# Half of a long depthwise convolution: three taps and the bias moved from VectorE to ScalarE and GpSimd, and a planner that holds back ScalarE table switches

## The chip, the cores and the metric

The kernel runs on one core of one Trainium2 chip. A core has five engines that run their own instruction queues beside each other: TensorE (PE in the profile, with PEld for its weight loads), VectorE (DVE), ScalarE (ACT), GpSimd (POOL) and SyncE (SP, which here only issues DMA transfers). The metric is the device time of one execution in microseconds. The time before is the median of three runs. The prediction is for the median after the change.

## The reference

The reference is a two-layer network in float32 on a sequence of 256 tokens with 1024 channels. Each layer is a feed-forward half step, a mixer, and another feed-forward half step, each between two RMS norms. The feed-forward part is `(silu(gate) * up) @ w2` with an inner width of 2816. The mixer of the second layer is a dilated attention in three patterns. The mixer of the first layer, the hybrid, is the one that the change touches:

```python
def conformer_conv(u, w_dw, b_dw, ln_g, ln_b):
    val, gate = jnp.split(u, 2, axis=-1)
    hid = causal_depthwise_conv(val * jax.nn.sigmoid(gate), w_dw, b_dw)
    return jax.nn.silu(layer_norm(hid, ln_g, ln_b))
...
def conv_ssd_mixer(...):
    proj = u @ w_in
    conv_in, z, xbc, dt_raw = jnp.split(proj, [s0, s1, s2], axis=-1)
    ya = conformer_conv(conv_in, ...)
    yb = mamba2_ssd(z, xbc, dt_raw, ...)
    return jnp.concatenate([ya, yb], axis=-1) @ w_out
```

The long convolution has 31 taps on each of 1024 channels: output at time t is the bias plus the sum over s from 0 to 30 of weight(30 - s) times the input at time t - s. The state space part (`mamba2_ssd`) has a short convolution of 4 taps with Silu behind it, on x, B and C; step sizes from a softplus; decays, which are exponentials of cumulated sums; and a gate `silu(z)`.

## The kernel before

**The matrix products.** Weights come from HBM in units of 128 x 2048 float32 (tile `raw`). ScalarE copies each unit into a rounded part (`wh`, type fp32r) and VectorE or GpSimd subtracts to get the rest (`wl`). Activations are split in the same way (`x`, `s`). A product is then three TensorE matmuls: high by high, high by low, low by high. All of these splits are in the queues of ScalarE, VectorE and GpSimd beside the other work. In the hybrid stage 17 units have their low part made on GpSimd (`GPSIMD_UNITS`).

**The order of the work.** The kernel's methods do not issue instructions. A `Recorder` notes each operation with what it reads and writes, and a planner puts them in an order for each engine before anything is issued. So every instruction in the profile has one line, L617, and an operation is known by its tiles (`wh<-raw` is a split, `t<-cv,chan,t` a convolution tap into PSUM bank `t`). The planner (`schedule`, L398) makes six turns. In each, `one_schedule` (L478) goes through time with costs for each operation (`cost`, L636) and chooses for each engine, in `choose` (L508), among the operations whose inputs are done and whose buffers can be had: of those that can start within `LOOK` (100 ns for VectorE and ScalarE) of the earliest, the one with the lowest rank. In the first turn the rank is the place in the program, shifted by `moved(...)`. In later turns it is a due time that `look_back` (L428) works out backwards from TensorE's order of the turn before. The turn with the shortest planned span is kept. Operations that start before `FIXED`, 35 us, keep their time of the first turn as their due time.

ScalarE's functions lie in tables: Exp, Silu and Sigmoid each need a table of their own, Copy, Identity and Square none (`TABLES`, L633). When an operation needs another table than the one loaded, an ACT_TABLE_LOAD stands ahead of it. The planner adds 1294 ns to its cost, and 3000 ns (`TABLE_TIME`) to its due time or 200 places to its rank.

**Buffers.** Tiles are of kinds, each with a fixed count. The kind `s`, 128 x 512 float32 in SBUF, has 17 buffers; `cv`, which holds the gated input of the long convolution (`glu`) and its result, has 5; in PSUM there are 4 banks `a`, 2 `w`, 1 `t` and 1 `c`. Buffers of a kind are given out in the order in which the program makes its tiles: a later one gets a buffer only when enough are free for the earlier ones without.

**The hybrid stage** (`hybrid`, L1178). The gated input of the long convolution is made as four tiles `glu[0]` to `glu[3]` of 2 x 128 channels by 256 tokens, the first two with tokens as rows and a transpose, the last two by `gated_feat` (L981), all with Sigmoid. In between stand the step sizes, which need Exp (`step_sizes`, L1139). `long_conv` (L1197) has two halves, `glu[0]` and `glu[1]`, then `glu[2]` and `glu[3]`. In each half the banks `t` and `c` hold the sums of one tile each. ScalarE starts a block with tap 1 and the bias (Identity with scale and bias from memory, 255 columns, L1207) and sets column 0 to the bias. VectorE adds the taps 2 to 30 in place in PSUM, one instruction `scalar_tensor_tensor` for each tap and block of 128 channels, and last tap 0, which writes the result to a `cv` tile (L1215). That is 30 VectorE instructions for each of the eight blocks.

Beside it run `xbc_pair` (L1223: projection, four taps of the short convolution, Silu) for B (`xbc_pair(4)`), C (`xbc_pair(5)`) and the four parts of x; `grow` (L1269) and `decays` (L1272: ScalarE scales a triangular matrix by each head's step, `s<-order,m`; a matmul cumulates; Exp follows, with a second small Exp `m<-a` for `left` in the first token tile); `gate_z` (Silu); and the products of the state space part. Behind both come `ln_half` (L1320: transposes of the convolution's result, then the layer norm) and the output projection.

Of the kernel before, what the change touches and what calls it, by code (L numbers as in the profile page):

```python
# [14 lines left out]
AF = mybir.ActivationFunctionType  # L15
ALU = mybir.AluOpType
# [3 lines left out]
P = 128  # L20
D = 1024
DFF = 2816
SEQ = 256
# [23 lines left out]
SECOND = 30  # L47
POOL_PIECE = 512
ON_POOL = (1, 1, 1)
CONV = (2000,1600)  # L50
GATE = 200
CONV_INIT = (-500, -100)
# [156 lines left out]
H_DW, H_DB, H_LG, H_LB, H_SW, H_SB = 0, 248, 256, 264, 272, 320  # L209
# [89 lines left out]
class Recorder:  # L299
# [81 lines left out]
    def together(self):  # L381
# [3 lines left out]
        head, rest = self.ops[at], self.ops[at + 1 :]  # L385
        head.cost += SWITCH
        for o in rest:
# [90 lines left out]
    def one_schedule(self):  # L478
# [18 lines left out]
        best = {}  # L497
        stale = set(free)

        def place_time(buf):  # L500
            kind = buf.kind
            ahead = 0
            for b in kind.bufs[kind.first : buf.index]:
                ahead += b.slot is None
            times = sorted(t for t in kind.free_at if t is not None)
            return times[ahead] if len(times) > ahead else None

        def choose(e):  # L508
            found = []
            low = None  # L510
            for o in cands[e]:
                s = max(free[e], ready[o.index])
                rank = o.rank if o.due is None else o.due
                if e == "scalar" and o.table and o.table != table:
                    rank += TABLE_RANKS if o.due is None else TABLE_TIME
                for b in o.bufs:
                    if b.slot is None:
                        t = place_time(b)
                        if t is None:
                            break  # L520
                        s = max(s, t + GAP)
                else:
                    found.append((rank, s, o))
                    if low is None or s < low:
                        low = s
            if low is None:
                return None
            return min((f for f in found if f[1] <= low + LOOK[e]), key=lambda f: f[:2])

        while len(order) < len(ops):  # L530
            for e in stale:
                best[e] = choose(e)
            stale = set()
            picks = [(b[1], e) for e, b in best.items() if b]
            assert picks, "no operation can start"
            s, e = min(picks)
            o = best[e][2]
            cands[e].remove(o)
            stale.add(e)
            for b in o.bufs:  # L540
# [38 lines left out]
            for u in users[o.index]:  # L579
                n = ops[u]  # L580
# [40 lines left out]
TURNS = 6  # L621
FIXED = 35000.0
TABLE_TIME = 3000.0
SWITCH = 280.0
TABLE_LOAD = 1294.0
TABLE_RANKS = 200
# [5 lines left out]
LOOK = {"tensor": 50.0, "vector": 100.0, "scalar": 100.0, "gpsimd": 0.0, "sync": 0.0}  # L632
# [71 lines left out]
class Kernel:  # L704
# [473 lines left out]
    def hybrid(self, xT, done):  # L1178
        nc = self.nc
        V = nc.vector  # L1180
        XD, XK, YZ = (nc.gpsimd if x else V for x in ON_POOL)
        chan = self.chan


        glu = []
# [7 lines left out]
        dt, a = self.step_sizes(xT)  # L1193
        for c in (2, 3):
            glu.append(self.gated_feat(xT, AF.Sigmoid))

        def long_conv():  # L1197
            out = []
            for j0 in (0, 2):
                acc = [self.ps([P, 2, SEQ], tag) for tag in "tc"]  # L1200
                part = lambda i: (acc[i % 2][:, i // 2, :], glu[j0 + i % 2][:, i // 2, :], 2 * (j0 + i % 2) + i // 2)
                tap = lambda ct, shift: chan[:, H_DW + ct * 31 + 30 - shift : H_DW + ct * 31 + 31 - shift]
                with nc.moved(CONV_INIT[j0 // 2]):
                    for i in range(4):
                        a, x, ct = part(i)
                        bias = chan[:, H_DB + ct : H_DB + ct + 1]
                        nc.scalar.activation(a[:, 1:], x[:, : SEQ - 1], AF.Identity, bias=bias, scale=tap(ct, 1))  # L1207
                        nc.scalar.activation(a[:, 0:1], bias, AF.Copy)
                o = [self.slot([P, 2, SEQ], tag="cv") for _ in range(2)]
                with nc.moved(CONV[j0 // 2]):  # L1210
                    for s in (*range(2, 31), 0):
                        for i in range(4):
                            a, x, ct = part(i)
                            to = a[:, s:] if s else o[i % 2][:, i // 2, :]
                            nc.vector.scalar_tensor_tensor(out=to, in0=x[:, : SEQ - s], scalar=tap(ct, s), in1=a[:, s:], op0=ALU.mult, op1=ALU.add)  # L1215
                for half in range(2):
                    out += [o[half][:, 0, :], o[half][:, 1, :]]
            return out

        hid = long_conv()  # L1220


# [177 lines left out]
        acc = [None] * NT  # L1400
# [309 lines left out]
```

## Time and profile before

| | |
|---|---|
| median of 3 runs | 1070.03 us (1068.65 to 1070.21) |
| profiled execution | 1070.98 us; its span from first to last instruction 1069.1 us |
| mean granted TensorE clock | 0.997 |
| instructions | 14980 |
| ACT_TABLE_LOAD | 18, mean 1283 ns |
| long convolution taps into bank `t` and into bank `c` | 116 each, mean 464 and 463 ns |
| bytes read from HBM | 194.51 MB, 183 GB/s over the span |

The profile is of one execution. A row of the view of busy time by windows gives the window, its length, then the busy time of PE, PEld, DVE, ACT and POOL with the number of their instructions in brackets, then the granted TensorE clock, the busy share of the DMA engines and GB/s. A row of the timeline gives start, duration, engine, line, operation, the tile written and those read, the shape and how many were merged; in square brackets stands how long the engine was idle before it and what ended that. A row of the groups gives the count behind the x, then busy time in all and the mean of one in ns, then idle time before them and who ended it. Starts of one engine lie closer together than durations, because its instructions overlap. The ends of matmuls are modelled, so a busy TensorE is not always one at its peak.

### The profile page before, as it was taken

What the parts mean: (1) busy time and instruction counts of PE and PEld (TensorE: products, weight loads), DVE (VectorE), ACT (ScalarE), POOL (GpSimd) and SP (SyncE); (2) the same over time, 40 slices, a digit from 0 to 9 for tenths busy, and PEclk for the clock granted to TensorE, in tenths of its full rate; (3) what the DMA queues carried; (4) which work ended last, traced back from release to release, by engine and by line L of the source; (5) the groups of instructions that cost most, each with busy time, mean ns of one, the idle gap of its engine ahead of it and who ended that gap; (6) DMA issues with size and microseconds to landing.
All of it is one profiled execution on the core that took longest, in us unless ns stands there. A gap on an engine that the chain in (4) does not pass through costs nothing.

```text
span 1069.1 us, 14980 instructions
## 1 busy us (share of the span) xinstructions
PE 1047.8 (98%) x5426; PEld 872.7 (82%) x5426; DVE 936.1 (88%) x1533; ACT 707.5 (66%) x1321; POOL 191.6 (18%) x167
## 2 busy tenths in 40 slices
PE   7999999998999999999999999999999999999997
PEld 5888888897877888888888888887888788888886
DVE  5799997789799999999979999998678769999993
ACT  6756666668785676666767666586577658476671
POOL 2410000296896040000003000001000413000000
PEclk9999999999999999999999999999999999999999
DMA  9573657454323532745654466383645232465451
GB/s 334 200 270 122 233 215 258 158 192 164 114 84 118 224 131 98 296 177 217 256 178 157 155 239 238 117 345 142 242 180 196 99 120 66 163 250 215 154 197 39
DMA packets 30633, 196.51 MB, mean 184 GB/s; under 512 B 3680, under 2 KB 4576, under 8 KB 8032
## 3 DMA queue, kind: packets, MB, share of 16 engines
q1 hardware_dynamic: 30560, 195.57, 50.3%
q8 instruction: 42, 0.69, 0.3%
q14 instruction: 31, 0.25, 0.1%
HBM read 194.51 MB, written 1.05 MB: 183 GB/s over the span
## 4 chain that ended last, share of the span: by engine, by line
PE 71%; DVE 2%; ACT 1%; issue 0%; POOL 0%; DVEq 0%; POOLq 0%; ACTq 0%
PE w L617 28%; PE a L617 26%; PE t L617 9%; PE c L617 7%; DVE wl L617 1%; ACT wh L617 0%; DVE s L617 0%; DVE y L617 0%; ACT x L617 0%; DVE h L617 0%; DVE x L617 0%; POOL m L617 0%; ACT junk L617 0%; DVEq L1706 0%; POOLq L1706 0%
## 5 line engine op out<-in xcount | busy, mean ns | idle before, releaser
L617 ACT ACTIVATE wh<-raw 128x512 fp32r<-128x512 f32 (+1 forms) x626 | 452.9, 774 | 157.7 <-DVE raw L617 51.9
L617 DVE TENSOR_TENSOR wl<-raw,wh 128x512 fp32r<-128x512 f32 (+1 forms) x554 | 483.3, 916 | 38.8 <-ACT wh L617 35.8
L617 PE MATMUL a<-wh,s 128*128 128x512 f32 x800 | 257.0, 392 | 0.0
L617 PE MATMUL w<-wh,x 128*128 128x512 f32 x600 | 197.1, 401 | 1.3 <-ACT x L617 0.8
L617 PEld LDWEIGHTS a<-wh,s 128*128 128x128 f32 x800 | 149.6, 188 | 33.6 <-ACT s L617 0.8
L617 PE MATMUL a<-wl,s 128*128 128x512 f32 x400 | 156.3, 391 | 0.0
L617 PE MATMUL w<-x,wh 128*128 128x512 f32 (+1 forms) x512 | 146.3, 352 | 1.3 <-DVE s L617 1.1
L617 POOL TENSOR_TENSOR m<-m,mhalf 128x1 f32<-128x1 f32 x28 | 18.9, 675 | 697.6 <-DVE m L617 697.6
L617 PEld LDWEIGHTS w<-wh,x 128*128 128x128 f32 x600 | 112.7, 190 | 27.0 <-ACT x L617 1.5
L617 PE MATMUL w<-wl,x 128*128 128x512 f32 x300 | 120.0, 401 | 0.0
L617 PE MATMUL w<-x,wl 128*128 128x256 f32 x400 | 112.4, 281 | 0.0
L617 DVE TENSOR_TENSOR raw<-raw,raw 128x1024 f32<-128x1024 f32 (+1 forms) x104 | 109.6, 1083 | 0.0
L617 PEld LDWEIGHTS w<-x,wh 128*128 128x128 f32 x512 | 89.4, 190 | 15.2 <-issue 2.4
L617 POOL TENSOR_TENSOR wl<-raw,wh 128x512 fp32r<-128x512 f32 x72 | 90.9, 1306 | 27.7 <-ACT wh L617 27.3
L617 PEld LDWEIGHTS a<-wl,s 128*128 128x128 f32 x400 | 75.2, 188 | 15.7
L617 PE MATMUL w<-wh,s 128*128 128x512 f32 x264 | 87.3, 391 | 0.0
L617 PEld LDWEIGHTS w<-x,wl 128*128 128x128 f32 x400 | 75.7, 189 | 1.5 <-issue 1.2
L617 PEld LDWEIGHTS w<-wl,x 128*128 128x128 f32 x300 | 57.1, 190 | 12.4 <-issue 0.9
L617 DVE SCALAR_TENSOR_TENSOR t<-cv,chan,t 128x254 f32<-128x254 f32 (+28 forms) x116 | 53.8, 464 | 6.7 <-ACT t L617 6.4
L617 PEld LDWEIGHTS w<-wh,s 128*128 128x128 f32 x264 | 49.6, 188 | 11.2 <-ACT s L617 0.5
L617 PE MATMUL t<-x,wh 128*128 128x512 f32 x160 | 58.0, 397 | 0.0
L617 PE MATMUL c<-x,wh 128*128 128x512 f32 x160 | 56.4, 393 | 0.0
(198 smaller groups left out, 1553.1 us busy)
## 6 DMA issues: line engine op xcount, KB each, us to landing
raw<-in_weights SPq DMA_DIRECT2D x176, 1024.0 KB, 4.9
g<-in_gains SPq DMA_DIRECT2D x11, 512.0 KB, 4.6
raw<-in_weights SPq DMA_DIRECT2D x8, 256.0 KB, 5.9
h<-in_x SPq DMA_DIRECT2D x4, 256.0 KB, 3.3
out<-h SPq DMA_DIRECT2D x4, 256.0 KB, 2.0
g<-in_consts SPq DMA_DIRECT2D x3, 192.0 KB, 2.4
chan<-in_chan SPq DMA_DIRECT2D x1, 170.0 KB, 9.3
order<-in_consts SPq DMA_DIRECT2D x1, 128.0 KB, 9.4
```

Source lines behind the costliest of these rows:

```text
L617: o.ins = f(*[real(a) for a in o.args], **{k: real(a) for k, a in o.kw.items()})
```

## The change

It has two parts.

In the planner, an operation of ScalarE that needs another table than the one loaded, and would start after `FIXED`, counts as starting 400 ns later (`TABLE_HOLD`) where the earliest start is looked for, where those within `LOOK` of it are picked out, and where the engine that goes next is chosen. Its real start is not moved.

In `long_conv`, for the second half alone (`SHARED = (0, 3)`), a new function `shared` makes taps 28, 29 and 30 of both tiles outside VectorE: ScalarE multiplies the shifted input by the tap's weight into an `s` tile (for tap 28 with the bias added, and the first 28 columns set to the bias), and GpSimd adds the three. ScalarE then copies the sum of each tile into its PSUM bank, in place of the start with tap 1. VectorE goes through taps 1 to 27 and 0. The operations of `shared` are moved by 500 places in the first turn. For the first half `n` is 0 and nothing changes.

```diff
--- before.py
+++ after.py
@@ -47,6 +47,8 @@
 SECOND = 30
 POOL_PIECE = 512
 ON_POOL = (1, 1, 1)
+SHARED = (0, 3)
+SHARED_RANKS = (2000, 500)
 CONV = (2000,1600)
 GATE = 200
 CONV_INIT = (-500, -100)
@@ -511,7 +513,9 @@
             for o in cands[e]:
                 s = max(free[e], ready[o.index])
                 rank = o.rank if o.due is None else o.due
+                held_up = 0.0
                 if e == "scalar" and o.table and o.table != table:
+                    held_up = TABLE_HOLD if s > FIXED else 0.0
                     rank += TABLE_RANKS if o.due is None else TABLE_TIME
                 for b in o.bufs:
                     if b.slot is None:
@@ -520,21 +524,21 @@
                             break
                         s = max(s, t + GAP)
                 else:
-                    found.append((rank, s, o))
-                    if low is None or s < low:
-                        low = s
+                    found.append((rank, s, o, s + held_up))
+                    if low is None or s + held_up < low:
+                        low = s + held_up
             if low is None:
                 return None
-            return min((f for f in found if f[1] <= low + LOOK[e]), key=lambda f: f[:2])
+            return min((f for f in found if f[3] <= low + LOOK[e]), key=lambda f: f[:2])
 
         while len(order) < len(ops):
             for e in stale:
                 best[e] = choose(e)
             stale = set()
-            picks = [(b[1], e) for e, b in best.items() if b]
+            picks = [(b[3], e) for e, b in best.items() if b]
             assert picks, "no operation can start"
-            s, e = min(picks)
-            o = best[e][2]
+            e = min(picks)[1]
+            s, o = best[e][1:3]
             cands[e].remove(o)
             stale.add(e)
             for b in o.bufs:
@@ -621,6 +625,7 @@
 TURNS = 6
 FIXED = 35000.0
 TABLE_TIME = 3000.0
+TABLE_HOLD = 400.0
 SWITCH = 280.0
 TABLE_LOAD = 1294.0
 TABLE_RANKS = 200
@@ -1194,25 +1199,55 @@
         for c in (2, 3):
             glu.append(self.gated_feat(xT, AF.Sigmoid))
 
+        def shared(j, at, n, whole):
+            first = None
+            for s in range(at, at + n):
+                a = self.slot([P, 2, SEQ])
+                for b in range(2):
+                    ct = 2 * j + b
+                    tap = chan[:, H_DW + ct * 31 + 30 - s : H_DW + ct * 31 + 31 - s]
+                    if first is None and whole:
+                        bias = chan[:, H_DB + ct : H_DB + ct + 1]
+                        nc.scalar.activation(a[:, b, s:], glu[j][:, b, : SEQ - s], AF.Identity, bias=bias, scale=tap)
+                        nc.scalar.activation(a[:, b, :s], bias.to_broadcast([P, s]), AF.Copy)
+                    else:
+                        nc.scalar.activation(a[:, b, s:], glu[j][:, b, : SEQ - s], AF.Copy, scale=tap)
+                if first is None:
+                    first = a
+                else:
+                    nc.gpsimd.tensor_tensor(out=first[:, :, s:], in0=first[:, :, s:], in1=a[:, :, s:], op=ALU.add)
+            return first
+
         def long_conv():
             out = []
             for j0 in (0, 2):
                 acc = [self.ps([P, 2, SEQ], tag) for tag in "tc"]
                 part = lambda i: (acc[i % 2][:, i // 2, :], glu[j0 + i % 2][:, i // 2, :], 2 * (j0 + i % 2) + i // 2)
                 tap = lambda ct, shift: chan[:, H_DW + ct * 31 + 30 - shift : H_DW + ct * 31 + 31 - shift]
+                n = SHARED[j0 // 2]
+                early = j0 == 2 and n
+                with nc.moved(SHARED_RANKS[j0 // 2]):
+                    some = [shared(j0 + p, 31 - n, n, early) for p in range(2 if n else 0)]
                 with nc.moved(CONV_INIT[j0 // 2]):
-                    for i in range(4):
+                    if early:
+                        for p in range(2):
+                            nc.scalar.activation(acc[p], some[p], AF.Copy)
+                    for i in range(0 if early else 4):
                         a, x, ct = part(i)
                         bias = chan[:, H_DB + ct : H_DB + ct + 1]
                         nc.scalar.activation(a[:, 1:], x[:, : SEQ - 1], AF.Identity, bias=bias, scale=tap(ct, 1))
                         nc.scalar.activation(a[:, 0:1], bias, AF.Copy)
                 o = [self.slot([P, 2, SEQ], tag="cv") for _ in range(2)]
                 with nc.moved(CONV[j0 // 2]):
-                    for s in (*range(2, 31), 0):
+                    for s in (*range(1 if early else 2, 31 - n), 0):
                         for i in range(4):
                             a, x, ct = part(i)
                             to = a[:, s:] if s else o[i % 2][:, i // 2, :]
                             nc.vector.scalar_tensor_tensor(out=to, in0=x[:, : SEQ - s], scalar=tap(ct, s), in1=a[:, s:], op0=ALU.mult, op1=ALU.add)
+                    if some and not early:
+                        for p in range(2):
+                            at = 31 - n
+                            nc.gpsimd.tensor_tensor(out=o[p][:, :, at:], in0=o[p][:, :, at:], in1=some[p][:, :, at:], op=ALU.add)
                 for half in range(2):
                     out += [o[half][:, 0, :], o[half][:, 1, :]]
             return out
```

## The prediction

> **What bounds the kernel now.** I read the page first (busy shares), then busy time by windows, then what TensorE (PE) waits for, then the ScalarE (ACT) order at the place where PE waits.
>
> ```profile
> PE 1047.8 (98%) x5426; PEld 872.7 (82%) x5426; DVE 936.1 (88%) x1533; ACT 707.5 (66%) x1321; POOL 191.6 (18%) x167
> ```
>
> PE is busy 98% of the span. The change takes no matmul away, so it can only gain where PE stands still or runs slowly. The windows say where that is:
>
> ```profile
> 240.00:250.00 10.00, 10.00 (x87) 10.00 (x86) 10.00 (x35) 6.25 (x12) 5.66 (x6) 1.00 0.40 145
> 275.00:280.00 5.00, 5.00 (x45) 5.00 (x44) 4.54 (x13) 2.73 (x6) 4.46 (x4) 1.00 0.06 25
> 330.00:335.00 5.00, 4.37 (x24) 3.42 (x23) 4.45 (x13) 4.39 (x14) 4.67 (x5) 1.00 0.59 208
> 365.00:740.00 375.00, 374.94 (x1781) 310.91 (x1780) 352.49 (x469) 247.65 (x410) 24.16 (x20) 1.00 0.55 201
> ```
>
> ```profile
> 250.00:255.00 5.00, 4.88 (x42) 4.70 (x41) 5.00 (x16) 2.94 (x8) 5.00 (x6) 1.00 0.55 184
> 255.00:260.00 5.00, 3.91 (x34) 3.73 (x33) 5.00 (x14) 5.00 (x16) 5.00 (x6) 1.00 0.59 206
> 260.00:265.00 5.00, 2.79 (x16) 1.70 (x14) 3.35 (x10) 4.94 (x11) 1.26 (x2) 0.99 0.57 213
> 265.00:270.00 5.00, 5.00 (x24) 3.82 (x24) 3.85 (x11) 4.95 (x8) 3.83 (x4) 0.67 0.08 31
> 270.00:275.00 5.00, 3.99 (x23) 2.83 (x23) 4.62 (x13) 3.42 (x10) 3.77 (x4) 1.00 0.52 185
> ```
>
> The columns after the length are busy time of PE, PEld, VectorE (DVE), ACT and GpSimd (POOL), then the granted clock. From 365 to 740 us, two feed-forward stages and more, PE misses 0.06 us of 375: a reordering there can win nothing. The hole is in the hybrid stage, 250 to 275 us: PE misses 0.12 + 1.09 + 2.21 + 0 + 1.01 = 4.43 us, and in 265 to 270 its clock is 0.67, which costs another 5 x 0.33 = 1.65 us. With the 0.63 us at 330 to 335 that makes 6.7 us, the most that the two edits can reach in this stage. In the worst ten microseconds ACT is busy 9.94 of 10. What ended PE's longer waits:
>
> ```profile
> 257.99 0.48 PE L617 MATMUL w<-x,wh 128*128 128x256 f32 x2 [1.09 <-DVE s L617]
> ...
> 262.04 0.44 PE L617 MATMUL a<-ident,s 128*128 128x128 f32 x2 [1.20 <-ACT s L617]
> ...
> 274.20 0.50 PE L617 MATMUL a<-x,wh 128*128 128x256 f32 x2 [1.01 <-ACT m L617]
> ...
> 331.91 0.63 PE L617 MATMUL w<-ident,v 128*128 128x128 f32 x4 [0.63 <-DVE x L617]
> ```
>
> **Edit one, the order: loads of tables.** The new rule holds an ACT operation that would need another table back by 400 ns against one that needs none, and the planner only takes what starts within 100 ns of the earliest. So as long as any operation without a table switch can start within 300 ns, the switch waits, whatever its due time. Before, only 3000 ns were added to its due time. Here is what ACT did in the hole:
>
> ```profile
> 260.06 1.28 ACT L617 ACT_TABLE_LOAD   x1
> 261.36 0.63 ACT L617 ACTIVATE s<-s 128x512 f32<-128x512 f32 x1
> 261.89 1.26 ACT L617 ACTIVATE s<-order,m 128x128 f32<-128x128 f32 x4
> 263.06 0.55 ACT L617 ACTIVATE s<-w,chan 128x256 f32<-128x256 f32 x1
> 263.62 1.28 ACT L617 ACT_TABLE_LOAD   x1
> 264.92 0.18 ACT L617 ACTIVATE m<-a 128x16 f32<-128x16 f32 x1
> 265.00 1.14 ACT L617 ACTIVATE wh<-raw 128x512 fp32r<-128x512 f32 x2
> 266.15 1.28 ACT L617 ACT_TABLE_LOAD   x1
> 267.45 0.63 ACT L617 ACTIVATE s<-s 128x512 f32<-128x512 f32 x1
> 267.99 1.14 ACT L617 ACTIVATE wh<-raw 128x512 fp32r<-128x512 f32 x2
> 269.14 1.28 ACT L617 ACT_TABLE_LOAD   x1
> 270.44 0.60 ACT L617 ACTIVATE s<-a 128x512 f32<-128x512 f32 x1
> ```
>
> Silu for the B channels (261.36), Exp for `grow` (264.92, 0.18 us), Silu for the C channels (267.45), Exp for the decays (270.44): four loads in ten microseconds, 4 x 1.28 = 5.1 us. `grow` is read only in the second token tile (L1367), and it stood ahead of four splits `wh<-raw` (265.00 and 267.99) that need no table. Under the new rule those of them whose weights have landed go first, and the Silu for C follows with its table still loaded. Two loads go, 2 x 1.28 = 2.57 us of ACT. What the Silu for C waits for besides is its last tap on DVE:
>
> ```profile
> 265.10 0.47 DVE L617 SCALAR_TENSOR_TENSOR s<-w,chan,s 128x253 f32<-128x253 f32 x1
> ```
>
> It ended at 265.57, so that Silu could start when the load of 266.15 began, 1.3 us earlier, and the Exp of the decays at about 266.15 + 0.63 + 1.28 = 268.1, 2.3 us earlier. PE's wait of 1.01 us at 274.20 ended with the small Exp that closes those decays; 2.3 us of lead covers all of it. What is late next there is the PE queue itself, since PE is full from 275 on. First term: -1.0 us.
>
> [...] The trace shows the load (1.28) and no drain: one of them ends at 266.15 + 1.28 = 267.43 and the Silu starts at 267.45. [...]
>
> What the rule can cost: it holds back the Silu for B too, on which PE waited at 262.04. Four `s<-order,m` (1.26 us, done behind it at 261.89) would now go ahead of it. I put that under the rivals, because the matmul order is planned anew as well and can fill the time.
>
> **The clock.** It fell to 0.67 of full over 265 to 270 after PE had missed 3.3 us of the ten before: half speed for 5 x 0.33 / 0.5 = 3.3 us. It falls or it doesn't, so the ends are 0 and -1.65 us; three of the waits ahead of it (1.09, 1.20 and the rest of 260 to 265) are not taken away by the missing loads. I take the middle, -0.8. [...]
>
> **Edit two, three taps to ACT and POOL.** For the second pair of channel tiles it adds on ACT 12 taps of 226 to 228 columns (4 of them with bias), 4 bias fills of 28 columns and 2 copies of 512 columns into PSUM, and removes 4 starts of 255 and 4 of one column. POOL gets 4 additions of 2 x 226 or 227 columns. DVE loses 12 taps of 226 to 228 columns and gets 4 of 255.
>
> ```profile
> L617 ACT ACTIVATE s<-order,m 128x128 f32<-128x128 f32 x32 | 10.3, 395 | 1.0 <-PE a L617 0.9
> ...
> L617 ACT ACTIVATE t<-cv,chan 128x255 f32<-128x255 f32 x4 | 2.2, 561 | 0.1
> ```
>
> ```profile
> L617 DVE TENSOR_TENSOR cv<-sg,w x4: 411/412/415, 234.0 to 253.3; 128x256 f32<-128x256 f32 x4
> ```
>
> ```profile
> L617 POOL TENSOR_TENSOR s<-s,s 128x512 f32<-128x512 f32 x8 | 10.2, 1283 | 1.5 <-ACT s L617 1.5
> ```
>
> ```profile
> L617 DVE SCALAR_TENSOR_TENSOR t<-cv,chan,t 128x228 f32<-128x228 f32 x4 | 1.8, 448 | 0.0
> ...
> L617 DVE SCALAR_TENSOR_TENSOR t<-cv,chan,t 128x254 f32<-128x254 f32 x2 | 1.0, 484 | 3.2 <-ACT t L617 3.2
> ```
>
> A tap on ACT lies between 395 ns (128 columns, scale from memory) and 561 (255, scale and bias): 8 x 0.48 + 4 x 0.56 = 6.1 us, the fills 4 x 0.2 to 0.4, say 0.8, the copies 2 x 0.60 = 1.2: 8.1 in all. Removed: 4 x 0.56 and 4 short ones of 0.2, 3.0. ACT gains 5 us net, somewhat less in a row because its instructions overlap (four of 395 ns took 1.26). The cover: the four products that make the two tiles (each of two blocks) start from 234.0 to 253.3, so the first tile is ready near 241, by even steps, and ACT had 10 - 6.25 = 3.75 us free in 240 to 250; the second is ready at 253.7, and ACT had 1.58 free in 270 to 275 and 2.27 in 275 to 280, beside the 2.57 us of loads. It fits, without much to spare. On POOL 4 x 1.28 = 5.1 us at most; it had 4.34 free in 240 to 250 and 3.74 in 260 to 265. A new wait comes with it: the copy into PSUM stands in ACT's queue behind POOL's last addition, and the weight splits stand behind the copy; POOL has little room in 275 to 280 (4.46 of 5 busy), so the addition has to be done before that, and I cost the wait at nothing on the strength of its 3.74 free us in 260 to 265 (without them, one addition, 1.28). Six tiles of kind `s`, of 17, are taken by the taps, and two of them stay until the copy; a shortage would hold back the decays, and its price is in rival A.
>
> DVE is relieved of 12 x 0.45 - 4 x 0.48 = 3.5 us, and its wait of 3.2 us before the second pair (it waited for eight ACT starts) shrinks to that for two copies. PE does not wait for the end of the convolution, since it is full in 335 to 340 and behind; I cost the relief itself at nothing. It passes on in two ways. The wait of 0.63 us at 331.91 hangs on a DVE step that stood among taps: with over 3 us of slack it should go, -0.6. And with the second pair due later, the taps of the first pair are due later too, so the short convolutions behind PE's wait of 1.09 us at 257.99 can go ahead of them: between 0 and -1.09, I take -0.5, as nothing in the code puts them ahead by itself.
>
> **Sum.** -1.0 - 0.8 - 0.6 - 0.5 = -2.9 us. The profiled execution took 1070.98 us (span 1069.1), 0.95 above the median of the runs shown, 1070.03; so 1068.1 on its own scale and 1067.1 on the median's.
>
> **Rivals.**
> A, the Silu for B is held up (slower). It now waits for all work that needs no table: 1.26 us of `s<-order,m`, and up to a pair's taps, 4 x 0.48 + 2 x 0.56 + 2 x 0.2 = 3.4 us, ready from 253.7 in a stretch where ACT is full. PE's transposes at 262.04 stand behind it, and the PSUM banks behind those. It decides once more than 2.1 us of such work is put ahead, for that is what the rest wins when the clock falls as before (1.0 + 0.6 + 0.5). Full price 1.26 + 3.4 = 4.7 us: 1070.03 - 2.1 + 4.7 = 1072.6. For it: ACT is busy 9.94 of 10 there. Against: the planner sees PE's wait and keeps the best of six turns.
> B, it moves nothing (same). The loads go, but PE's wait for Exp turns into one for DVE, which is also full at 250 to 260, and the clock falls as before. Then 0.6 or less is left: 1069.4. The case that the loads stay in the same number gives the same.
> C, the hole closes. With the loads gone, the order planned anew has room to fill all of it: 1070.03 - 6.7 = 1063.3. Against: three of its waits belong to DVE or to the unavoidable first Silu.
> D, POOL's additions block DVE. In 250 to 260 POOL was busy without a break and DVE got through 16 + 14 instructions, one each 0.33 us, which it could not do if a POOL instruction of 1.28 us shut it out. So I give it little: 5.1 us more on DVE instead of 3.5 less takes the last two terms back, 1070.03 - 1.0 - 0.8 = 1068.2. [...]
>
> **How the numbers follow.** Forecast (around 1067.1, from 1066 to 1067.9) 0.37, C and what lies between 0.13, B 0.27, A 0.21, D 0.02. What a measurement of this kernel can tell from no change is about 0.2%, 2.1 us. Faster than 1067.9 are the forecast and C, 0.50; the same B and D, 0.29; slower A, 0.21. The range reaches from C's 1063.3 to just past A's 1072.6, to 1073; beyond each end, where a second stretch of half clock (1.65) or a gain outside the stage would lie, I leave about one in ten.
>
> **What would show it.** Right: two loads fewer between 255 and 275; the Silu for C before the Exp of `grow`; no PE wait on a small Exp near 272; the wait near 332 gone; DVE with no 3 us wait before the second pair; PE full outside 250 to 275 as before. Wrong: PE waiting on ACT near 262 for 2 us or more with taps ahead of the Silu (A); as many loads as before, or the same 4.4 us of PE idle time under other names (B).

## The result, and the profile after

| | before | after |
|---|---|---|
| median on the same chip | 1070.12 us (1068.1 to 1070.58, 6 runs) | 1063.1 us (1061.76 to 1064.04, 6 runs) |
| profiled execution, its span | 1070.98, 1069.1 us | 1062.56, 1060.8 us |
| table loads | 18 | 14 |

The ratio is 0.9938 (95% interval 0.9925 to 0.9951): 7 us faster, where 3 were forecast. First the busy shares of the changed kernel, then its windows. (The line that is L617 in the kernel before is L621 in the changed kernel, and L618 to L623 in the kernels of the experiments.)

```profile
PE 1044.7 (98%) x5426; PEld 871.1 (82%) x5426; DVE 933.9 (88%) x1525; ACT 706.3 (67%) x1327; POOL 195.3 (18%) x171
```

```profile
250.00:255.00 5.00, 5.00 (x45) 5.00 (x44) 4.96 (x14) 4.97 (x15) 5.00 (x5) 1.00 0.57 210
255.00:260.00 5.00, 5.00 (x45) 5.00 (x44) 4.91 (x14) 4.82 (x11) 4.97 (x5) 1.00 0.62 197
260.00:265.00 5.00, 4.33 (x27) 3.09 (x26) 4.75 (x14) 4.78 (x8) 5.00 (x5) 1.00 0.62 223
265.00:270.00 5.00, 5.00 (x28) 3.36 (x27) 5.00 (x15) 2.42 (x8) 5.00 (x5) 1.00 0.59 215
270.00:275.00 5.00, 5.00 (x38) 4.66 (x37) 4.45 (x13) 4.38 (x9) 4.75 (x5) 1.00 0.00 0
...
330.00:335.00 5.00, 5.00 (x23) 4.12 (x23) 5.00 (x16) 2.04 (x5) 0.00 (x0) 1.00 0.57 210
```

Of the 4.43 us that PE missed in these 25 us, 0.67 are left, the 0.63 us at 330 to 335 are gone, and the clock stays at 1.00. That is 3.76 + 0.63 + 1.65 = 6.0 us. Over the whole stage PE now misses 1.06 us of 165; before it was 5.38 (the row of before, then that of after):

```profile
200.00:365.00 165.00, 159.62 (x984) 136.43 (x983) 145.55 (x387) 118.67 (x250) 114.37 (x95) 0.99 0.40 142
```

```profile
200.00:365.00 165.00, 163.94 (x1012) 139.87 (x1011) 148.87 (x387) 119.75 (x260) 118.32 (x99) 1.00 0.45 160
```

Outside it the two profiles differ by 0.8 us at the start and 1 us in the last feed-forward stage. Neither seems to be this change's. PE's product `t<-ident,y` starts at 202.48 us before and at 201.69 after; in two_loads_back and taps_again_first below, whose order up to there is that of the changed kernel, it starts at 200.25 and 203.59. The last feed-forward stage is shorter by 0.8 us in the control named neutral as well, and by 1.0 in exp_behind, whose order there is that of the kernel before.

ACT in the hole, after:

```profile
259.06 1.14 ACT L621 ACTIVATE wh<-raw 128x512 fp32r<-128x512 f32 x2
260.22 1.28 ACT L621 ACT_TABLE_LOAD   x1
261.51 1.15 ACT L621 ACTIVATE s<-s 128x512 f32<-128x512 f32 x2
262.57 0.55 ACT L621 ACTIVATE s<-w,chan 128x256 f32<-128x256 f32 x1
263.13 1.28 ACT L621 ACT_TABLE_LOAD   x1
264.43 0.18 ACT L621 ACTIVATE m<-a 128x16 f32<-128x16 f32 x1
264.77 0.60 ACT L621 ACTIVATE s<-a 128x512 f32<-128x512 f32 x1 [0.16 <-PE a L621]
```

The Silus of B and C stand together (261.51, two instructions), then `grow` and the decays: two loads instead of four. For the two Silus to stand together C must be ready by 262. What made that so is DVE's order. The first taps of B's short convolution, before and after:

```profile
254.34 0.48 DVE L617 SCALAR_TENSOR_TENSOR s<-w,chan,s 128x255 f32<-128x255 f32 x1
```

```profile
248.11 0.47 DVE L621 SCALAR_TENSOR_TENSOR s<-w,chan,s 128x255 f32<-128x255 f32 x1
...
257.90 0.48 DVE L621 SCALAR_TENSOR_TENSOR s<-a,chan,s 128x253 f32<-128x253 f32 x1
```

B starts 6 us earlier (0.8 of them are the earlier start of the stage), and C's last tap ends at 258.38; before it ended at 265.57. The other end of DVE's work is the long convolution's. The windows from its first tap on DVE to its last result, before and after:

```profile
217.60:345.70 128.10, 123.04 (x809) 106.50 (x808) 118.75 (x320) 93.15 (x199) 104.79 (x86) 0.99 0.39 140
```

```profile
216.80:337.50 120.70, 119.95 (x804) 104.22 (x803) 116.86 (x313) 91.80 (x205) 109.23 (x90) 1.00 0.42 148
```

This chain (DVE is the third of the busy times) is 118.75 us of work and 9.35 idle before, 116.86 and 3.84 after. The idle time fell more than the work. One piece of it is the start of the second pair, before:

```profile
285.62 0.49 DVE L617 SCALAR_TENSOR_TENSOR t<-cv,chan,t 128x254 f32<-128x254 f32 x1 [3.20 <-ACT t L617]
```

After, its first tap (279.90) starts behind the last of the first pair with no wait.

At its end the chain has little room, and that was so before the change too. PE takes the convolution's first tile 0.45 us after it is done (344.11 + 0.85 = 344.96) in the kernel before, and 0.37 us after (335.89 + 0.85 = 336.74, taken at 337.11) in the changed one:

```profile
344.11 0.85 DVE L617 SCALAR_TENSOR_TENSOR cv<-cv,chan,t 128x256 f32<-128x256 f32 x2
...
345.41 0.38 PE L617 MATMUL t<-ident,cv 128*128 128x128 f32 x2
```

### The profile page after: what moved, and what is told of

It reads as the page before. It is cut to its first block, busy times and chain, and to the rows that moved or that the text cites. A ratio compares the mean times of both kernels' runs of the same rounds, so it can differ in the third digit from the quotient of the medians.

```text
span 1060.8 us, 14991 instructions
## 1 busy us (share of the span) xinstructions
PE 1044.7 (98%) x5426; PEld 871.1 (82%) x5426; DVE 933.9 (88%) x1525; ACT 706.3 (67%) x1327; POOL 195.3 (18%) x171
## 4 chain that ended last, share of the span: by engine, by line
PE 94%; DVE 2%; ACT 2%; issue 1%; DMA 0%; POOL 0%; SPq 0%; DVEq 0%; POOLq 0%; ACTq 0%
PE w L621 40%; PE a L621 32%; PE t L621 12%; PE c L621 9%; ACT wh L621 1%; DVE wl L621 0%; DMA raw<-in_weights 0%; DVE y L621 0%; DVE h L621 0%; ACT junk L621 0%; POOL m L621 0%; ACT x L621 0%; ACT L621 0%; SPq L621 0%; DVE s L621 0%
## 5 line engine op out<-in xcount | busy, mean ns | idle before, releaser
L621 ACT ACTIVATE wh<-raw 128x512 fp32r<-128x512 f32 (+1 forms) x626 | 452.6, 775 | 146.4 <-DVE raw L621 51.8
L621 DVE TENSOR_TENSOR wl<-raw,wh 128x512 fp32r<-128x512 f32 (+1 forms) x554 | 483.0, 917 | 37.2 <-ACT wh L621 34.8
L621 PE MATMUL a<-wh,s 128*128 128x512 f32 x800 | 257.3, 393 | 0.0
L621 PE MATMUL w<-wh,x 128*128 128x512 f32 x600 | 198.2, 402 | 1.4 <-ACT x L621 0.9
L621 PEld LDWEIGHTS a<-wh,s 128*128 128x128 f32 x800 | 149.6, 188 | 33.5 <-ACT s L621 1.0
L621 PE MATMUL a<-wl,s 128*128 128x512 f32 x400 | 156.3, 391 | 0.0
L621 POOL TENSOR_TENSOR m<-m,mhalf 128x1 f32<-128x1 f32 x28 | 18.7, 671 | 698.2 <-DVE m L621 698.2
L621 PE MATMUL w<-x,wh 128*128 128x512 f32 (+1 forms) x512 | 143.8, 348 | 0.1
L621 PEld LDWEIGHTS w<-wh,x 128*128 128x128 f32 x600 | 112.6, 189 | 27.2 <-issue 1.8
L621 PE MATMUL w<-wl,x 128*128 128x512 f32 x300 | 119.1, 398 | 0.0
L621 PE MATMUL w<-x,wl 128*128 128x256 f32 x400 | 112.4, 281 | 0.0
L621 DVE TENSOR_TENSOR raw<-raw,raw 128x1024 f32<-128x1024 f32 (+1 forms) x104 | 109.7, 1083 | 0.0
L621 PEld LDWEIGHTS w<-x,wh 128*128 128x128 f32 x512 | 88.4, 188 | 12.3 <-DVE pt L621 0.4
L621 POOL TENSOR_TENSOR wl<-raw,wh 128x512 fp32r<-128x512 f32 x72 | 90.9, 1298 | 17.8 <-ACT wh L621 17.6
L621 PEld LDWEIGHTS a<-wl,s 128*128 128x128 f32 x400 | 75.2, 188 | 16.0
L621 PE MATMUL w<-wh,s 128*128 128x512 f32 x264 | 87.2, 391 | 0.0
L621 PEld LDWEIGHTS w<-x,wl 128*128 128x128 f32 x400 | 75.3, 188 | 1.3 <-issue 1.0
L621 PEld LDWEIGHTS w<-wl,x 128*128 128x128 f32 x300 | 56.9, 190 | 12.6 <-issue 0.7
L621 PEld LDWEIGHTS w<-wh,s 128*128 128x128 f32 x264 | 49.6, 188 | 11.1 <-ACT s L621 0.5
L621 PE MATMUL t<-x,wh 128*128 128x512 f32 x160 | 57.8, 396 | 0.0
L621 PE MATMUL c<-x,wh 128*128 128x512 f32 x160 | 56.5, 393 | 0.0
L621 DVE SCALAR_TENSOR_TENSOR t<-cv,chan,t 128x254 f32<-128x254 f32 (+29 forms) x112 | 52.2, 466 | 3.6 <-ACT t L621 3.2
```

Source lines behind the costliest of these rows:

```text
L621: o.ins = f(*[real(a) for a in o.args], **{k: real(a) for k, a in o.kw.items()})
```

## The experiments

Two theories stood at first. **L**: the four table loads made the hole, and the two that are gone are the gain. **S**: DVE's order made it; with fewer taps to do, B, C and the step sizes went ahead of the first pair's taps, and the loads are covered. The first eight kernels of the table brought a third, **D**: PE meets two bounds one behind the other, the hole at 255 to 275 and the end of the convolution near 337 to 345, and a gain at the first is lost at the second unless that moves too. Its rival **E**: DVE's chain bounds the whole stage in both kernels.

The results, each as a ratio to the kernel before on the same chip (the changed kernel has 0.9938, 0.9925 to 0.9951). The last columns are of the profiled run: the length of DVE's chain, from its first long tap to the convolution's last result, and DVE's busy and idle time in it, from the same view as above.

| kernel | median us | ratio, 95% interval | loads | chain | busy | idle |
|---|---|---|---|---|---|---|
| hold_only | 1068.81 | 0.9988, 0.998 to 0.9996 | 14 | 125.6 | 119.2 | 6.4 |
| taps_only | 1067.02 | 0.9973, 0.9963 to 0.9983 | 18 | 123.5 | 117.1 | 6.4 |
| exp_behind | 1069.47 | 0.9994, 0.9984 to 1.0003 | 16 | 126.4 | 118.6 | 7.8 |
| bc_sooner | 1065.48 | 0.9959, 0.9946 to 0.9971 | 16 | 125.1 | 118.4 | 6.7 |
| two_loads_back | 1066.64 | 0.9966, 0.9954 to 0.9979 | 16 | 126.5 | 117.0 | 9.5 |
| taps_again_late | 1067.45 | 0.9978, 0.997 to 0.9987 | 14 | 124.8 | 120.7 | 4.1 |
| taps_again_first | 1066.26 | 0.996, 0.9948 to 0.9973 | 14 | 123.2 | 120.3 | 2.9 |
| neutral | 1069.18 | 0.9994, 0.9985 to 1.0003 | 20 | 126.5 | 118.9 | 7.6 |
| taps_out_before | 1069.2 | 0.9993, 0.9983 to 1.0002 | 18 | 125.2 | 115.9 | 9.3 |
| taps_out_after | 1062.53 | 0.9933, 0.9921 to 0.9945 | 14 | 117.8 | 114.0 | 3.8 |
| hold_sooner | 1064.49 | 0.9951, 0.9938 to 0.9964 | 14 | 122.4 | 118.5 | 3.9 |
| four_taps | 1063.55 | 0.9946, 0.9934 to 0.9958 | 14 | 119.3 | 115.2 | 4.1 |

**The two edits, one at a time.** The rule without the taps:

```diff
-SHARED = (0, 3)
+SHARED = (0, 0)
```

> The planner's 400 ns alone; the convolution stays whole on VectorE. Theory L (loads: the table loads in the full stretch of ScalarE made the hole): at least two loads fewer between 255 and 275 us, TensorE's idle time there falls from 4.4 us to 2 or less and the clock stays up, 3 to 5 us faster than before (1065 to 1067). Theory S (slack: three taps fewer on VectorE let the taps of B and C and the step sizes go ahead of the first half of the long convolution): the waits of TensorE on VectorE and on the first Silu near 258 to 264 us stay, 0 to 2 us faster (1068 to 1070).

It won 1.2 us. It has the 14 loads of the full change in all, but three between 255 and 275 us, where the kernel before has four and the changed one two. And it still has the hole:

```profile
261.81 0.37 PE L621 MATMUL a<-m,order 128*128 128x16 f32 x2 [2.77 <-ACT wh L621]
263.31 0.44 PE L621 MATMUL a<-ident,s 128*128 128x128 f32 x2 [1.13 <-ACT s L621]
```

B's last tap on DVE, and ACT in the stretch:

```profile
254.55 0.47 DVE L621 SCALAR_TENSOR_TENSOR s<-a,chan,s 128x253 f32<-128x253 f32 x1
```

```profile
260.16 1.15 ACT L621 ACTIVATE wh<-raw 128x512 fp32r<-128x512 f32 x2
261.33 1.28 ACT L621 ACT_TABLE_LOAD   x1
262.62 0.63 ACT L621 ACTIVATE s<-s 128x512 f32<-128x512 f32 x1
```

B was ready at 255.02, but its Silu came at 262.62, behind splits and `s<-order,m`, and PE's 1.13 us ended with it. (The 2.77 us are put down to the splits that ended at 261.31; the matmul reads none of them, so what released it is open.) A held Silu of B is the mechanism of rival A; how much of the lost gain is its price, and how much belongs to the open 2.77 us, is not shown. L asked for two loads fewer in the stretch and there was one, so this run alone doesn't decide on L.

The taps without the rule:

```diff
-TABLE_HOLD = 400.0
+TABLE_HOLD = 0.0
```

> Three taps and the bias of the second half on ScalarE and GpSimd alone; the hold is 0, so the planner chooses as before. Theory L: as many table loads as before, so the hole stays; 1 us faster from the waits near 258 and 332 us (1069). Theory S: B's and C's taps start some 5 us earlier on VectorE, the waits near 258 to 264 us go although the loads stay; 4 to 6 us faster (1064 to 1066).

It won 2.9 us with all 18 loads. One PE wait was left in the hole, and a slow clock behind it:

```profile
269.56 0.47 PE L621 MATMUL w<-wh,x 128*128 128x512 f32 x1 [2.48 <-DVE s L621]
```

```profile
270.00:275.00 5.00, 5.00 (x31) 4.95 (x30) 3.83 (x11) 0.85 (x3) 3.76 (x4) 0.66 0.53 179
```

The two parts give 4.1 us by themselves and 7 together (4.2 and 6.6 by the ratios). Neither theory foresaw a sum that is larger than its parts.

**The step on `grow`.** The kernel before in its own order; the Exp of `grow` goes behind the Silu of C, and a Copy takes its operand out of PSUM at its old place:

```diff
+                if o is self.late:
+                    self.tc.nc.scalar.activation(extra, real(o.args[1]), AF.Copy)
+                    continue
...
+                if o is self.behind:
+                    self.tc.nc.scalar.activation(real(self.late.args[0]), extra, AF.Exp, scale=-1.0)
```

> The order of before, instruction by instruction, but for one: where the Exp of grow stood, a Copy without a table takes its input out of PSUM (so the bank comes free at the same place), and the Exp itself stands behind the Silu of C. Two table loads of 1.28 us go, nothing else is planned anew. Theory L: the Silu of C and the Exps of the decays come 1.3 to 2.3 us earlier, TensorE's wait of 1.0 us near 274 goes, 1 to 2.6 us faster (1067.5 to 1069). Theory S: the holes ahead of it stay and with them the half clock; 0 to 1 us faster.

Two loads fewer in the stretch, and nothing won that can be measured. The wait that L said would go is still there: PE waits on the small Exp, and ACT on PE.

```profile
271.01 0.50 PE L621 MATMUL a<-x,wh 128*128 128x256 f32 x2 [1.00 <-ACT m L621]
```

```profile
264.12 0.63 ACT L621 ACTIVATE s<-s 128x512 f32<-128x512 f32 x1 [0.95 <-DVE s L621]
...
268.94 0.60 ACT L621 ACTIVATE s<-a 128x512 f32<-128x512 f32 x1 [1.14 <-PE a L621]
```

(This is one of its two shortest executions; the end says more of it.) C's Silu waited for its last tap, and the decays' Exp for PE's own products, which stand in a fixed place of PE's queue. Time freed on ACT went nowhere.

**B and C sooner, nothing else.** The kernel before, whose planner counts the short taps of B and C as due 6 us sooner:

```diff
-                rank = o.rank if o.due is None else o.due
+                rank = o.rank if o.due is None else o.due - o.sooner
...
+                    nc.ops[-1].sooner = SOONER if j in (4, 5) else 0.0
```

> The kernel before, but in the planner the VectorE taps of B and C count as due 6 us sooner, so that they go ahead of the first half's long taps. No tap is moved off VectorE and there is no hold. Theory L: the loads stay about as they are, so at most the wait of 1.1 us near 258 us goes, 1069. Theory S: that order is what the change brought about; TensorE's waits near 258 to 264 us go, 3 to 5 us faster (1065 to 1067).

It won 4.5 us with no tap moved and no table held: more than the rule alone, and by the medians more than the taps alone, though those two intervals overlap. So the main effect, B and C ahead of the long taps, can be had without the change.

**Doubled costs in the changed kernel's order.** A small Exp between the two Silus, which brings two loads more (16 in all instead of 14):

```diff
+                if o is self.marked:
+                    self.tc.nc.scalar.activation(extra, extra, AF.Exp)
```

> The changed kernel's order, but with a small Exp of one scratch column on ScalarE between the Silu of B and the Silu of C, so that two table loads more stand there (16 instead of 14), about 2.6 us of ScalarE. Theory L (the loads made the hole): PE waits behind them again, the time rises by 2 to 4 us over the changed kernel, to 1065 to 1067. Theory S (room on VectorE made it, the loads are mostly covered): since B and C are ready from 252.8 and 258.4 and PE takes the Silus' result only from 261 on, at most 1 us more: 1063 to 1064.2. If PE's wait brings the lower clock back, about 3 us come on top of either.

The ratio went from 0.9938 to 0.9966, 3 us. The lower clock came back with it (0.50 over 265 to 270, shown at the end), and with the 3 us that the author had estimated on top for that case the time of 1066.6 is what S gives (1066 to 1067.2), less than L's (1068 to 1070). The trace speaks for L all the same: S had the loads covered, and PE waits 3.02 us for the Silu of C behind them. So with B and C in time the Silus are what PE waits for, and the 3 us are the loads and the slow clock together.

```profile
264.19 2.08 PE L623 MATMUL a<-s,s 128*128 128x128 f32 x8 [3.02 <-ACT s L623]
```

Eight taps of the second pair, then eight of the first, done twice (the second time into a scratch buffer):

```diff
+                if o.index in self.again:
+                    kw = {k: real(a) for k, a in o.kw.items()}
+                    self.tc.nc.vector.scalar_tensor_tensor(**{**kw, "out": extra[:, : o.kw["in1"].free_size()]})
...
+                            if early and s in (26, 27):
+                                nc.again.add(nc.ops[-1].index)
```

> The changed kernel's order, with 8 taps of the second pair of channel tiles done a second time into a scratch buffer on VectorE, about 3.6 us more work there, late in the stage. It gives back the load that the change took off VectorE, at the place where it was taken off. Theory S in its plain form (what counts is only that B and C go ahead of the first pair's taps, the load behind that is covered): 0 to +0.5 us over the changed kernel, 1063 to 1063.6. The rival (the relief itself is worth its time, the end of the convolution holds PE): +2 to +3.6 us, 1065 to 1066.7.

4.3 us by the ratios. PE, which had found the result of the convolution ready at 337.11 in the changed kernel, now waits for it:

```profile
338.22 0.39 PE L622 MATMUL a<-wh,x 128*128 128x512 f32 x1
342.13 0.69 PE L622 MATMUL t<-ident,cv 128*128 128x128 f32 x2 [3.52 <-DVE cv L622]
```

```profile
337.11 0.38 PE L621 MATMUL t<-ident,cv 128*128 128x128 f32 x2
```

(The last row is the changed kernel's, its tile done at 335.89 + 0.85 = 336.74.) The room there was 0.4 us. Eight taps done twice made the chain 4.1 us longer, and PE lost 3.5 and then ran at half clock (0.50 in each microsecond from 341 to 347). (The profiled execution, 1070.22 us, is the slowest of eleven; the others took 1065.8 to 1068.1.)

> The changed kernel's order, with 8 taps of the first pair done a second time into a scratch buffer on VectorE, about 3.6 us more work there, early in the stage. Theory S: whatever of it stands ahead of B's and C's short convolutions and the step sizes makes them later; they had 4 to 6 us of lead after the change, so 0 to +2 us, and up to 3 us more if PE's wait brings the lower clock back. Theory L (VectorE doesn't matter there): 0 to +0.3 us.

2.4 us by the ratios, without a slow clock (1.00 over 218.7 to 341.9). DVE's work rose by 3.4 us and its chain by 2.5: at the early place the load counts as well. But it counts at another place than S had named. PE's wait is for DVE's product that makes a gated input, 1.63 us that the changed kernel doesn't have, while B's Silu costs PE no more than there (0.39 us against 0.59):

```profile
242.40 0.50 PE L622 MATMUL w<-x,wh 128*128 128x256 f32 x2 [1.63 <-DVE cv L622]
```

**A control.** The kernel before with one of the planner's constants changed by a trifle:

```diff
-GAP = 100.0
+GAP = 101.0
```

> A control: the kernel before, with the planner's allowance between a buffer's last use and its next one 101 ns instead of 100, which changes the plan here and there with no intent. It shows how far a new plan alone moves the time. If plans scatter by less than 1 us, the effects of 1.2 to 7 us of the other runs are those of their edits: 1069 to 1071. If a new plan by itself is worth 3 us or more either way, the single edits can't be read as causes.

No difference that can be measured, with a new plan and even two loads more. It is one plan, so how far plans scatter is not shown; but it makes it unlikely that differences of 3 us and over are the luck of a plan. The 1.2 of hold_only is near what this can do.

**Fewer taps.** The kernel before and the changed one, each in its own order, without 8 taps of the second pair:

```diff
+                if o.index in self.left_out:
+                    continue
...
+                            if j0 == 2 and s in (26, 27):
+                                nc.left_out.add(nc.ops[-1].index)
```

> The kernel before, in its own order, with 8 taps of the second pair of channel tiles (shifts 26 and 27) left out on VectorE, some 3.6 us of its work; the long convolution then misses these taps, the rest of the work is the same. Theory D (two bounds one behind the other: PE loses its time in 255 to 275, and is full from there on, so it comes to the convolution's result by itself): 0 to -0.6 us, 1069.3 to 1069.9. Rival E (VectorE's chain of taps bounds the whole stage in the kernel before): about -3.5 us, 1066.4.

> The changed kernel, in its own order, with the same 8 taps left out (the output misses them). Theory D: the moved taps were enough, PE is the bound again: 0 to -0.7 us, 1062.4 to 1063.1. Rival E: about -3.5 us, 1059.6. Beside the run with the same 8 taps doubled (+4.3) it says on which side of the balance the changed kernel lies.

Both chains are 2.9 us shorter, and neither time moves: 0.9993 against 1, and 0.9933 against 0.9938, with intervals that overlap. The chain of the first:

```profile
217.30:342.50 125.20, 120.22 (x795) 104.19 (x794) 115.91 (x312) 91.89 (x197) 104.77 (x86) 0.99 0.40 143
```

and its waits of PE:

```profile
PE a L619 <- ACT s L619: 1.2, 1, 1.2
PE a L619 <- ACT m L619: 1.0, 1, 1.0
PE w L619 <- DVE s L619: 1.0, 1, 1.0
```

They are those of the kernel before, none gone. E falls: in the order of either kernel, work taken off DVE's end is worth nothing that can be measured. With its order held, the changed kernel loses 4.3 us with 8 taps more there and wins nothing with 8 fewer, as D has it. That does not set it apart from the kernel before, which has the same small room at that place (0.45 us); taps were not doubled there.

**The order without the taps.** The rule, and B and C sooner:

```diff
-SHARED = (0, 3)
+SHARED = (0, 0)
...
+SOONER = 6000.0
```

> The new rule for table switches together with B's and C's short convolutions counted as due 6 us sooner, and no tap moved off VectorE. Theory D: PE's hole closes nearly as in the changed kernel, but the convolution, with all its taps, then holds PE at its end: VectorE's chain from its first tap to the convolution's end would take the 118.8 us of work of the kernel before and the 3.8 us idle of the changed one, 5.5 us less than before, 1064.5; 1064 to 1066, short of the changed kernel. Theory L (the loads are what matters once B and C are early): 1063, the same as the changed kernel.

The forecast of D, 1064.5, was met in number: 1064.49. The work on DVE is that of before, the idle time that of the changed kernel:

```profile
215.90:338.30 122.40, 119.75 (x802) 103.95 (x801) 118.51 (x321) 87.60 (x193) 105.08 (x87) 1.00 0.41 146
```

But the mechanism of D isn't there, so the number is luck. The convolution does not hold PE: its first tile is done at 336.66 + 0.86 = 337.52 and taken at 338.06, without a wait. PE loses its time in the hole, 0.77 and 1.71 us against 0.59 in the changed kernel:

```profile
252.77 0.48 PE L622 MATMUL w<-x,wh 128*128 128x256 f32 x2 [0.77 <-ACT s L622]
...
260.61 0.48 PE L622 MATMUL w<-x,wh 128*128 128x256 f32 x2 [1.71 <-ACT wh L622]
```

```profile
338.06 0.38 PE L622 MATMUL t<-ident,cv 128*128 128x128 f32 x2
```

With all its taps the convolution came forward together with PE, as it did in bc_sooner, where no such wait stands either. It is 1.4 us short of the changed kernel, at the edge of what the intervals separate. Against bc_sooner the rule gave 0.8, which they don't separate.

**More taps.** `SHARED = (0, 4)`:

> The changed kernel with four taps of the second pair on ScalarE and GpSimd instead of three. Theory D: PE is full already, so nothing more is won, 1062.3 to 1064. Rival E: VectorE loses four more taps of 0.45 us, -1.8 us, 1061.3.

The chain got 1.4 us shorter, the time did not fall (0.9946). No kernel tried beat the changed one beyond its interval.

## Why the prediction was right in direction and short in size

**Where.** The hole at 250 to 275, the clock in it and the wait at 332 are where the gain came from, and nothing came from 365 to 740. The measured 1063.1 is below the forecast's 1066 to 1067.9 and next to rival C's price, 1063.3, which was the low end of the range (by the ratio, 0.9938 of 1070.03, it is 1063.4). C was given 0.13 together with what lies between, on the ground that three of its waits belong to DVE or to the first Silu. The waits did belong to DVE; what was wrong was to think that the change did not touch them.

**The table loads, -1.0.** The count was right: two of the four went, and the Silus stood as described. What failed is that 2.3 us of lead on ACT would cover PE's wait on the small Exp. exp_behind gave ACT those two loads in the old order, and the wait stayed at 1.00 us, since the Exp of the decays waited for PE. It also missed that `grow`, "read only in the second token tile", frees a PSUM bank, which by the code the decays need next, so that in the old order it couldn't just move back; that was not measured. In the new order the two loads are worth 3 us, the slow clock that they bring included (two_loads_back). What a load cost here was not its duration but whether the Silu behind it had its input.

**The clock, -0.8.** The middle between 0 and -1.65 was taken; all of it came, as far as the mean clock tells: 0.999 in every run of the changed kernel.

**The wait at 332, -0.6.** Gone, as forecast, but the relief of DVE was not needed for it: in bc_sooner, with all taps on DVE, PE misses 0.13 us in all from 325 to 335, and in neutral 0.29 us. So the cause that was given is not shown, and that the size came out is luck.

**B and C ahead, -0.5.** This is the term that was mis-sized most. "Nothing in the code puts them ahead by itself": the planner's due times did. B began 6 us earlier, and with it went the wait of 1.09, half of the 1.20 behind it, the rest of 260 to 265, and the slow clock. bc_sooner has this alone, with one wait of 2.53 us and a slow clock left (0.50 over 258 to 260), and won 4.5 us.

**The relief of DVE, nothing.** True in the order of before (taps_out_before). What it is worth in the new one, beyond letting B and C go first, is open. taps_again_late lost 4.3 us, but it made the chain 4.1 us longer in an order that had been planned without that work; hold_sooner, planned with all taps on DVE, is 1.4 us short of the changed kernel, and PE doesn't wait for the convolution there. The reason given was too weak in any case: PE was full at 335, but it took the convolution's result 0.45 us after it was done, so a queue that the other terms bring 6 us forward needs the chain to come forward too. The size was off as well: 3.5 us by mean durations of 0.45. Taps start 0.36 to 0.37 us apart, so 8 taps are 2.9 us (taps_out_after), and DVE's chain lost 1.9. The wait of 3.2 us, which was expected to shrink, went altogether.

**The costs on ACT and POOL.** A shared tap took 0.47 to 0.58 us (forecast 0.48 to 0.56), a fill 0.21, a copy into PSUM 0.60:

```profile
L621 ACT ACTIVATE s<-cv,chan 128x228 f32<-128x228 f32 x4 | 2.3, 577 | 1.5 <-DVE cv L621 1.5
...
L621 ACT ACTIVATE s<-cv,chan 128x227 f32<-128x227 f32 x4 | 1.9, 471 | 0.0
...
L621 ACT ACTIVATE s<-chan 128x28 f32<-128x28 f32 x4 | 0.8, 209 | 0.0
```

In all ACT's busy time fell by 1.2 us and POOL's rose by 3.7, and from 240 us on PE's only wait on ACT in the stage is 0.59 us at 262.20.

**The rivals.** A's mechanism is seen in hold_only, though not slower than before on the whole. B's outcome, that loads go and nothing moves, is what exp_behind shows, but the wait did not turn into one for DVE: PE still waited for the Exp, and the Exp for PE. D (POOL blocks DVE) fails: with POOL busy 5.00 and 4.97 of 5 us (250 to 260 in the changed kernel), DVE's taps still start 0.37 us apart.

## What to carry to other kernels

An idle hole on the fullest engine names the first bound only. Before a relief is costed at nothing because PE is full where it would be felt, shift PE's queue by what the other terms win and ask which transfer, tap or Silu would then be late: here the convolution's end had 0.4 us to spare, before as well as after. And the worth of an edit hangs on the order around it. Moving what feeds the late instruction (B and C) won 4.5 us by itself; two table loads were worth nothing in the old order and 3 us in the new one; the load of DVE, beyond letting B and C go first, cost time when it was added to a fixed order, but was not shown to be worth more than 1.4 us to a planner that can place it. A time that comes out as forecast is no proof of the mechanism: hold_sooner met its number with the wait in another place.

## What the runs showed of the hardware

Where the lower clock of PE was seen, it came with waits of 1 to 3.5 us, and in stretches of about 3.4 and 6.8 us. With a wait of 2.53 us (bc_sooner) and one of 3.02 us (two_loads_back) it went to half, 0.50; in hold_sooner a wait of 1.71 us left it at 1.00. The length of a stretch follows from the share of each window (a clock of 0.86 over 5 us is half clock for 5 x 0.14 / 0.5 = 1.4 us). In two_loads_back it is 1.4 + 5 + 0.4 = 6.8 us:

```profile
260.00:265.00 5.00, 1.40 (x8) 1.00 (x6) 1.83 (x5) 4.92 (x8) 4.38 (x4) 0.86 0.64 213
265.00:270.00 5.00, 5.00 (x11) 2.75 (x11) 4.12 (x11) 2.02 (x5) 1.27 (x1) 0.50 0.58 210
...
270.00:271.00 1.00, 1.00 (x3) 0.42 (x2) 1.00 (x4) 0.38 (x3) 0.54 (x1) 0.80 0.00 0
```

and in bc_sooner 0.7 + 2 + 0.7 = 3.4 us:

```profile
256.00:258.00 2.00, 1.81 (x13) 1.84 (x14) 2.00 (x7) 1.97 (x4) 2.00 (x3) 0.83 0.43 86
258.00:260.00 2.00, 2.00 (x11) 2.00 (x11) 1.76 (x5) 1.50 (x4) 1.91 (x2) 0.50 0.90 373
260.00:262.00 2.00, 2.00 (x16) 2.00 (x16) 0.64 (x2) 1.24 (x3) 0.00 (x0) 0.82 0.17 70
```

The same sum gives 0.1 + 3.3 = 3.4 us in the kernel before (0.99 over 260 to 265, 0.67 over 265 to 270), 3.4 us in taps_only (0.66 over 270 to 275), and 0.3 + 6 + 0.5 = 6.8 us in taps_again_late, where PE waited 3.52 us (0.84 over 340 to 341, 0.50 to 347, 0.75 to 348). With the shorter waits of the kernel before, the clock fell in two profiles and not in two others. That of taps_out_before has 1.2, 1.0, 1.0, 0.7 and 0.3 us, and its clock fell to 0.94 and 0.72 over 260 to 265 and 265 to 270, again 0.6 + 2.8 = 3.4 us. The profile of exp_behind has nearly the same waits of PE as that of the kernel before (1.2, 1.0, 1.0, 0.7 and 0.3 us against 1.2, 1.1, 1.0, 0.7 and 0.3), and in that of neutral PE misses 4.45 us from 250 to 275, against 4.43; the clock stays at 1.00 over this stretch in both, and in that of the kernel before it fell to 0.67.

Two of the twelve executions of exp_behind took 1066.5 us at a mean clock of 0.999 or 1.000, the others 1068.2 to 1070.8 at 0.995 to 0.998. The profiled one is of the two, and its span is 4.7 us shorter than that of the kernel before. The clock is not all of it: 1.6 us are there by PE's product at 200.90 (202.48 before), another 1.6 come between there and the one at 328.69 (331.91 before), where the stretch at half clock stood, and most of the rest in the last feed-forward stage. The changed kernel, with one wait of 0.59 us, keeps a mean clock of 0.999 in all six runs.
